# Attention over sequences of unequal length: ScalarE copies pair 2 in two-tile halves, and SyncE reads two rows of its table at once

## The chip, the core and the metric

The kernel runs on one NeuronCore of a Trainium2 chip. The core has TensorE (PE: matmuls, and weight loads, PEld), VectorE (DVE), ScalarE (ACT), GpSimd (POOL) and SyncE (SP), which issues most of the DMAs. The engines run their own instruction streams and wait for each other on semaphores. The metric is the device time of one execution in microseconds.

## What is computed

32 sequences of 64 to 511 valid rows, 8 heads of 64 columns. Rows past a sequence's length are zero in the output.

```python
for b in range(batch):                       # 32
    x_b = x[b, :lengths[b]]                  # up to 512 rows x 512
    q, k, v = np.split(x_b @ w_qkv, 3, axis=-1)          # each split into 8 heads of 64
    scores = 64 ** -0.5 * (q @ k.T)          # per head
    attn = softmax(scores)                   # per row
    output[b, :lengths[b]] = attn @ v        # heads side by side
```

## The kernel before

The sequences are sorted by length, longest first, and taken two at a time. A pair gets a class N (its length rounded up to 32 rows) and T = N/128 rounded up, the number of 128-row tiles. For every class there is a body with two halves, one for each sequence of the pair (h = 0, 1). While half h runs the attention of its sequence, it projects the next sequence, g = 1 - h. All engines have a copy of each body and branch to it by the class, which they read from a table.

Inside a half the heads go in four pairs. What TensorE does, in order, is a string of tokens; for T = 2:

```python
2: "S S B0 b1 A0 A1 B2 S S V1 b3 A2 O A3 R3 X3 V0",
```

`S` is the scores of one pair (pairs 1, 2, 3 of this sequence, then pair 0 of the next), whose exponential ACT takes. `B` and `b` project Q and K of one pair of the next sequence into one bank of PSUM, a0 and a1 in turn; a capital means that DVE copies the bank to `qkT`, a small letter that ACT does. `V` projects one tile of V into such a bank, and DVE copies it to `v_aug` (where the last tile has up to 64 rows, in two instructions, lines 531 and 532). `A` is attention times V of one pair into the area `pav`. The results of A0 and A1, and of A2 and A3, are normalised together by DVE (a reciprocal, then two multiplications): the first norm behind A1, the second at `R3 X3`. `O` is ACT's store of the first two pairs' output.

A group waits on a semaphore `e_<bank>` until the last reader of its bank is through (`acquire`), and raises `f_<bank>_<engine>` for the engine that reads it. So `b3` waits until the copy of `B2` has freed a0, `V0` until the copy of `V1` has freed a1, and `b1` of the next half until the copy of `V0` has. `A2` writes the area that the first norm reads. Before the change it has no wait of its own for that: `b3` stands ahead of it on TensorE and waits for a copy that stands behind the norm on DVE.

SP moves the data. In a two-tile half it waits until TensorE is done with the old xT (`s_xtf`), transposes the next x (two DMAs, line 1379), stores two pairs of output (line 1302) and loads x for a later sequence (lines 1390 and 1394). Which sequences these are it reads from a table in SBUF, `steps`, one row of four registers for each half (`read_step`, lines 1474 and 1475): an address step and a blocking `TENSOR_LOAD`. `steady` is the path of most two-tile bodies, without branches inside. One-tile bodies take their transposes through a staging area (line 1513), from which GpSimd copies them to xT (line 1710).

Of the kernel before, what the change touches and what calls it, by code (L numbers as in the profile page):

```python
# [152 lines left out]
def kernel(  # L153
# [9 lines left out]
    B, MAXS, D = x.shape  # L163
# [7 lines left out]
    def sb(name, shape, dt):  # L171
        return nc.alloc_sbuf_tensor(name, shape, dt).ap()

    def sem(name):
        return tc.alloc_semaphore(name)
# [20 lines left out]
    rank = sb("rank", [B, 1], FP32)  # L196
# [11 lines left out]
    steps = sb("steps", [1, B, 4], I32)  # L208
# [62 lines left out]
    halves_av = ("v0", "v1")  # L271
# [3 lines left out]
    free = {b: sem(f"e_{b}") for b in banks + halves_av + ("x0",)}  # L275
# [6 lines left out]
    def acquire(pr, b):  # L282
        if pr.busy.get(b):
            pr.take("pe", free[b])
            pr.busy[b] = False
# [262 lines left out]
    def attnv(pr, h, i, T, late=False, b=None, qts=None):  # L548

        for s_ in ("s0", "s1"):  # L550
            if pr.pair[s_] == i or T == 1 and pr.pair[s_] is not None:
                acquire(pr, s_)
        for v in halves_av if b is None else (b,):
            acquire(pr, v)
        va = v_aug[h]
        if b is not None:
            jobs = [(2 * 74 * k, i, qt) for k, qt in enumerate(qts)]
        elif T == 1:
            jobs = [(74 * 2 * j, j, 0) for j in range(NPAIR)]
        elif T == 4:  # L560
            jobs = [(256 * qt, i, qt) for qt in range(T)]
        else:
            jobs = [(74 * (4 * qt + 2 * (i % 2)), i, qt) for qt in range(T)]
        mms = []
        for o0, j, qt in jobs:
            for par in range(2):
                o = o0 + par * (HD + 1 if T == 4 and b is None else 74)
                into = pav if b is None else area[b]
                for kt in range(T):
                    mms.append(  # L570
                        mm(
                            into[:, o : o + HD + 1],
                            ep[:, j, par, kt, qt * P : (qt + 1) * P],
                            va[:, kt, 2 * j + par, :],
                            kt == 0,
                            kt == T - 1,
                        )
                    )
        if b is None and T in (2, 3) and i % 2 == 0:
            acquire_carry(pr, mms)  # L580
            return
        on = onat[h]
        if b is not None:
            n = len(qts)
            res = into[:, 0 : 2 * 74 * n].rearrange("p (t a d) -> p t a d", a=2, d=74)
            dst = on[:, i // 2, qts[0] : qts[0] + n, P * (i % 2) : P * (i % 2 + 1)]
            dst = dst.rearrange("p t (a d) -> p t a d", d=HD)
            sh, fin = [n, 2], i % 2 == 1 and T - 1 in qts
        elif T == 4:
            res = pav.rearrange("p (j n) -> p j n", n=256)[:, :, 0 : 2 * (HD + 1)]  # L590
            res = res.rearrange("p j (a d) -> p j a d", d=HD + 1)
            dst = on[:, i // 2, :, P * (i % 2) : P * (i % 2 + 1)]
            dst = dst.rearrange("p t (a d) -> p t a d", d=HD)
            sh, fin = [NT, 2], i % 2 == 1
        else:
            sh, fin = [2, 4] if T == 1 else [T, 4], True
            res = pav[:, 0 : 74 * sh[0] * 4].rearrange("p (b j d) -> p b j d", j=4, d=74)
            if T == 1:
                dst = on[:, :, 0, :].rearrange("p b (j d) -> p b j d", d=HD)
            else:  # L600
                dst = on[:, i // 2, 0:T, :].rearrange("p t (a d) -> p t a d", d=HD)
        r0 = 2 * qts[0] if b is not None else 0
        rv = rcp[:, i, r0 : r0 + sh[0] * sh[1]].rearrange("p (j a) -> p j a", a=sh[1])
        num, den = res[..., 0:HD], res[..., HD]
        name = "av" if b is None else b
        close(pr, name, "dve", mms, False)
        each = T == 4 or b is not None

        def recip():
            opens = i % 2 == 0 and (b is None or 0 in qts)  # L610
            for j in (0, 1) if T == 1 else (i // 2,) if not each or opens else ():
                pr.take("dve", s_od[h][j], 16)
            pr.take("dve", full[(name, "dve")])
            pr.add("dve", lambda e: e.reciprocal(out=rv, in_=den).then_inc(s_r, 1))  # L614

        def mult():
            pr.take("dve", s_r)

            if T == 1:
                cuts = [(slice(0, 2), 0)]  # L620
            elif b is not None:
                whole = [] if h else [k for k, t in enumerate(qts) if t < T - 1]
                cuts = [(slice(0, len(whole)), None)] if whole else []
                cuts += [(slice(k, k + 1), t) for k, t in enumerate(qts) if k not in whole]
            elif h == 0:
                cuts = [(slice(0, T - 1), None), (slice(T - 1, T), T - 1)]
            else:
                cuts = [(slice(t, t + 1), t) for t in range(T)]

            def fn(e):  # L630
                for w, t in cuts:
                    ops = dict(
                        out=dst[:, w], in0=num[:, w],
                        in1=rv[:, w].unsqueeze(3).broadcast_to(list(num[:, w].shape)),
                    )
                    if t is None:
                        ins = e.tensor_tensor(op=ALU.mult, **ops)
                    else:
                        ins = e.scalar_tensor_tensor(  # L639
                            scalar=now[0][:, 1, t : t + 1], op0=ALU.mult, op1=ALU.mult, **ops  # L640
                        )
                if fin:
                    ins.then_inc(s_of[h][i // 2], 1)
                if b is not None:
                    if fin:
                        ins = e.memset(small, 0.0)
                    ins.then_inc(free[b], 1)

            pr.add("dve", fn)
            if b is not None:  # L650
                pr.busy[b] = True

        todo = {"R": recip, "X": mult}
        if not late:
            for fn in todo.values():
                fn()
        return todo
# [5 lines left out]
    def spread_last(pr):  # L663
# [15 lines left out]
    ORDER = {  # L679
# [3 lines left out]
    }  # L683
    DENSE = "K2 q2 D E1 E3 I1 H3 D k0 c A0 Q0~ A1 D V2 O V1 A2 D A3~ V0"
    FOUR = "S E1 S G1 S E2 S G2 S E0 S E3 S G0 G3 S S A0 Z0 V1 +A1 S S Z1 V3 +A2 S O S V0 +Z2 S A3 Z3 S S V2"
# [648 lines left out]
    with nc.Block() as block:  # L1334

        @block.sync
        def _(e):
# [11 lines left out]
            rank = e.alloc_register("rank")  # L1349
# [90 lines left out]
            for more in range(EARLY):  # L1440
# [7 lines left out]
            cur = regs[e.engine][1]  # L1448
            steps_r = [
                [e.alloc_register(f"{r}{h}") for r in ("ahead", "own", "steady")] for h in range(2)  # L1450
            ]
            steps_r = [[ahead, cur, own, flag] for ahead, own, flag in steps_r]
# [17 lines left out]
                    e.reg_mov(owed, 0)  # L1470
                nc.switch_bb(out_, parent=top)

            def read_step(h):
                e.reg_load(steps_r[h], steps[
                    0:1, bass.ds(e.snap(rank, min_val=0, max_val=B - 1), 1), :])

            def steady(N):

                k, top = CLASSES.index(N), nc.cur_bb
                yes, no = f"even_b{N}", f"even_x{N}"  # L1480
                e.br_cmp(steps_r[0][3], CLASSES.index(P), yes, no, "IS_LT")
                nc.switch_bb(yes, parent=top)
                for h in range(2):
                    if h:
                        read_step(h)
                    wait_dec(e, s_xtf[h])
                    to_xT(h, N, 2)
                    if h == 0:
                        pay_owed(f"{N}e", False)
                    else:  # L1490
                        pay(0)
                    wait_dec(e, s_xc[1 - h])
                    load(1 - h, 5, N, index(h, 0))
                    e.reg_add(rank, rank, 1)
                e.reg_mov(owed, 1)
                e.reg_mov(flat, 1)
                e.br_cmp(cur, k, f"sp_b{k}", f"even_z{N}", "IS_EQ")
                nc.switch_bb(f"even_z{N}", parent=top)
                e.br(f"sp_x{k}")
                nc.switch_bb(no, parent=top)  # L1500
# [50 lines left out]
            def body(e, N):  # L1551
                T = -(-N // P)
                read_step(0)
                if T == 1:
                    staged(N)
                if T == 2:
                    steady(N)
                for h in range(2):
                    if h:
                        read_step(h)  # L1560
                    top = nc.cur_bb
                    lab, out_ = f"trans_b{N}_{h}", f"trans_x{N}_{h}"
# [265 lines left out]
```

## Time and profile before

| | |
|---|---|
| median of 3 runs | 339.34 us (339.07 to 339.44) |
| the profiled execution | 338.92 us; its span, first to last instruction, 337.2 us |
| granted TensorE clock, mean | 0.994 |
| busy: PE, DVE, ACT, POOL | 321.1, 209.9, 243.0, 67.8 us |
| two-tile halves | 12, from 237.5 to 315.5 us of the span |
| one-tile halves | from 315.5 us to the end |

How to read the rows: in a timeline a row has its start and its length in us, the engine, the line, the operation and the tiles (out <- in), and in brackets how long the engine idled before it and what ended that. Rows of groups have `x` and a count, busy us, mean ns of one, and the idle time ahead of the group. `PEq` and `SPq` are the engines' sequencers; line 306 is the helper that writes every matmul, line 61 and line 1294 are those that write waits. Rows of one line give the shortest, the median and the longest duration in ns. In rows of waits stand the total, the count and the longest in us.

### The profile page before, as it was taken

What the parts mean: (1) busy time and instruction counts of PE and PEld (TensorE: products, weight loads), DVE (VectorE), ACT (ScalarE), POOL (GpSimd) and SP (SyncE); (2) the same over time, 40 slices, a digit from 0 to 9 for tenths busy, and PEclk for the clock granted to TensorE, in tenths of its full rate; (3) what the DMA queues carried; (4) which work ended last, traced back from release to release, by engine and by line L of the source; (5) the groups of instructions that cost most, each with busy time, mean ns of one, the idle gap of its engine ahead of it and who ended that gap; (6) DMA issues with size and microseconds to landing.
All of it is one profiled execution on the core that took longest, in us unless ns stands there. A gap on an engine that the chain in (4) does not pass through costs nothing. (4 is left out here: it accounts for less than half of the span.)

```text
span 337.2 us, 12374 instructions
## 1 busy us (share of the span) xinstructions
PE 321.1 (95%) x4390; PEld 207.9 (62%) x4391; DVE 209.9 (62%) x578; ACT 243.0 (72%) x345; POOL 67.8 (20%) x126
## 2 busy tenths in 40 slices
PE   6999999999999999999999999999999999999881
PEld 2664554465656566565666666777768777777660
DVE  3676567455566567467557655865666667677651
ACT  4578788788888987887977888787767575665531
POOL 3634020202020220220222022202123111313150
PEclk9999999999999999999999999999999999999997
DMA  6966799856555976997788969695897557876522
GB/s 213 352 151 223 194 360 256 309 177 208 169 201 155 259 294 152 260 318 227 218 272 286 216 203 316 184 238 172 228 215 191 161 167 160 201 147 179 174 79 71
DMA packets 82273, 72.11 MB, mean 214 GB/s; under 512 B 40652, under 2 KB 63180, under 8 KB 82196
## 3 DMA queue, kind: packets, MB, share of 16 engines
q1 hardware_dynamic: 70340, 59.61, 63.6%
q10 hardware_dynamic: 11856, 11.54, 9.9%
q8 instruction: 40, 0.66, 0.9%
q14 instruction: 37, 0.30, 0.3%
HBM read 25.32 MB, written 36.70 MB: 184 GB/s over the span
## 5 line engine op out<-in xcount | busy, mean ns | idle before, releaser
L348 ACT ACTIVATE ep<-psc 128x704 f16<-128x704 f32 (+7 forms) x193 | 157.0, 861 | 55.9 <-PE psc L306 38.1
L306 PE MATMUL pa<-xT,w_r 128*128 128x224 f16 (+21 forms) x984 | 122.9, 275 | 5.0 <-PEq L61 3.4
L306 PEld LDWEIGHTS pa<-xT,w_r 128*128 128x128 f16 (+1 forms) x984 | 71.9, 97 | 33.5 <-issue 13.4
L412 DVE CAST qkT<-pa 128x512 f16<-128x512 f32 (+9 forms) x73 | 41.5, 570 | 45.5 <-PE pa L306 42.6
L306 PE MATMUL psc<-qkT 64*128 64x352 f16 (+17 forms) x702 | 68.3, 287 | 0.8 <-PEq L61 0.3
L306 PE MATMUL pa<-w_r,xT 128*128 128x512 f16 (+4 forms) x332 | 57.9, 330 | 0.0
L306 PE MATMUL pav<-v_aug,ep 128*128 128x65 f16 x1254 | 55.0, 194 | 0.4 <-PEq L61 0.4
L306 PEld LDWEIGHTS pav<-v_aug,ep 128*128 128x128 f16 x1254 | 49.0, 98 | 9.0 <-issue 1.6
L306 PE MATMUL pav<-xT,w_r 64*128 64x352 f16 (+12 forms) x392 | 50.8, 307 | 0.0
L380 ACT ACTIVATE ep<-psc 128x960 f16<-128x960 f32 (+3 forms) x48 | 43.4, 961 | 8.8 <-PE psc L306 6.0
L639 DVE SCALAR_TENSOR_TENSOR onat<-pav,masks,rcp 128x128 f32<-128x128 f32 (+2 forms) x124 | 44.4, 396 | 5.0 <-DVE rcp L614 1.9
L1666 POOL MEMSET v_aug<- 128x256 f16 x24 | 7.5, 314 | 187.5 <-POOLq L1294 187.5
L306 PEld LDWEIGHTS psc<-qkT 64*128 64x128 f16 x702 | 26.8, 94 | 28.2 <-issue 18.3
L1660 POOL CAST x<-x_nat 128x1536 f16<-128x1536 f32 (+3 forms) x33 | 42.0, 1272 | 8.0 <-POOLq L1294 7.7
L411 ACT CAST qkT<-pa 128x352 f16<-128x352 f32 (+8 forms) x62 | 28.7, 468 | 15.6 <-ACTq L61 7.8
L435 DVE TENSOR_TENSOR v_aug<-pa,masks 128x512 f16<-128x512 f32 (+1 forms) x46 | 30.7, 672 | 13.8 <-PE pa L306 13.5
L306 PEld LDWEIGHTS pav<-xT,w_r 64*128 64x128 f16 (+1 forms) x392 | 26.6, 94 | 12.3 <-issue 1.3
L306 PEld LDWEIGHTS pa<-w_r,xT 128*128 128x128 f16 (+2 forms) x332 | 22.7, 99 | 16.2 <-issue 4.1
L614 DVE RECIPROCAL rcp<-pav 128x8 f32<-128x8 f32 (+2 forms) x69 | 13.5, 196 | 22.5 <-PE pav L306 16.6
L306 PE MATMUL pav<-w_r,xT 128*128 128x512 f16 (+3 forms) x124 | 26.9, 350 | 0.0
L306 PEld LDWEIGHTS pa<-v_aug,ep 128*128 128x128 f16 x538 | 19.7, 98 | 7.1 <-issue 2.9
L306 PE MATMUL pa<-v_aug,ep 128*128 128x65 f16 x538 | 22.3, 194 | 0.0
(84 smaller groups left out, 169.1 us busy)
## 6 DMA issues: line engine op xcount, KB each, us to landing
out_dram<-zt SPq DMA_DIRECT2D x16, 768.0 KB, 6.0
x_nat<-in_x_dram SPq DMA_DIRECT2D x12, 512.0 KB
x_nat<-in_x_dram SPq DMA_DIRECT2D x5, 1024.0 KB
out_dram<-onat ACTq DMA_DIRECT2D x12, 384.0 KB, 4.9
out_dram<-onat SPq DMA_DIRECT2D x12, 384.0 KB, 4.5
x_nat<-in_x_dram SPq DMA_DIRECT2D x17, 256.0 KB, 5.7
out_dram<-onat ACTq DMA_DIRECT2D x16, 256.0 KB, 3.3
x_nat<-in_x_dram SPq DMA_DIRECT2D x4, 768.0 KB
```

Of the source, the lines that this page charges most:

```text
L306: return lambda e: e.matmul(o, lhsT, rhs, start=start, stop=stop)
L348: lambda e: e.activation(out=dst, in_=src, func=AF.Exp, scale=scale),
L380: lambda e, par=par, b=b: e.activation(out=ep[:, i, par, 0:3, 0:N], in_=psc_f[:, par, 0 : 3 * N].rearrange("p (t n) -> p t n", n=N), func= ...
L411: return lambda e: e.copy(out=dst, in_=src)
L412: return lambda e: e.tensor_copy(out=dst, in_=src)
L435: return lambda e: e.tensor_tensor(out=v_aug[h][:, t, lo // HD : lo // HD + n, 0:HD], in0=area[b][:, 0:w].rearrange("p (a d) -> p a d", d=HD),
L614: pr.add("dve", lambda e: e.reciprocal(out=rv, in_=den).then_inc(s_r, 1))
L639: ins = e.scalar_tensor_tensor(scalar=now[0][:, 1, t : t + 1], op0=ALU.mult, op1=ALU.mult, **ops)
L1660: e.tensor_copy(out=x16[h][:, 0:T, :], in_=x_nat[h][:, 0:T, :]).then_inc(s_xc[h], 1)
L1666: e.memset(v_aug[h][:, T - 1, NPAIR:NH, 0:HD], 0.0)
```

## The change

Three edits, all for T = 2:

1. `B2` becomes `b2`: the copy of pair 2 of Q and K goes from DVE to ACT.
2. The first norm of a half (i = 1) ends with a memset of one element on DVE that raises the semaphore of `v0`, a half of `pav`; the next user of the area on TensorE, `A2`, waits for it.
3. SP reads both rows of `steps` at the top of a two-tile body, the second one into spare registers. At the start of the second half two register moves take the place of the read.

```diff
@@ attnv @@
+        back = halves_av[0] if b is None and T == 2 and i == 1 else b
...
-                if b is not None:
+                if back is not None:
                     if fin:
                         ins = e.memset(small, 0.0)
-                    ins.then_inc(free[b], 1)
+                    ins.then_inc(free[back], 1)
 
             pr.add("dve", fn)
-            if b is not None:
-                pr.busy[b] = True
+            if back is not None:
+                pr.busy[back] = True
@@ ORDER @@
-        2: "S S B0 b1 A0 A1 B2 S S V1 b3 A2 O A3 R3 X3 V0",
+        2: "S S B0 b1 A0 A1 b2 S S V1 b3 A2 O A3 R3 X3 V0",
@@ sync @@
-            def read_step(h):
-                e.reg_load(steps_r[h], steps[
-                    0:1, bass.ds(e.snap(rank, min_val=0, max_val=B - 1), 1), :])
+            def read_step(h, at=None, into=None):
+                at = rank if at is None else at
+                e.reg_load(into or steps_r[h], steps[
+                    0:1, bass.ds(e.snap(at, min_val=0, max_val=B - 1), 1), :])
+
+            def read_second():
+                e.reg_add(second[3], rank, 1)
+                read_step(1, second[3], [second[0], cur] + second[1:3])
+
+            def take_second():
+                for k, r in ((0, second[0]), (2, second[1])):
+                    e.reg_mov(steps_r[1][k], r)
+
+            second = [e.alloc_register(f"{r}_second") for r in ("ahead", "own", "steady", "rank")]
@@ steady @@
                     if h:
-                        read_step(h)
+                        take_second()
@@ body @@
                 if T == 2:
+                    read_second()
                     steady(N)
                 for h in range(2):
-                    if h:
+                    if h and T == 2:
+                        take_second()
+                    elif h:
                         read_step(h)
```

The places that the prediction speaks of, in the second half of the body of class 192 when the next pair has class 160. On DVE, from the first norm to the copies of `V1`, before:

```order
L614 RECIPROCAL rcp<-pav 128x8 [waits s_od10,f_av_dve]
L639 ISA [waits s_r]
L639 SCALAR_TENSOR_TENSOR onat_1<-pav,masks,rcp 128x256
L639 ISA
L639 SCALAR_TENSOR_TENSOR onat_1<-pav,masks,rcp 128x256
L412 CAST qkT_0<-pa 128x2x160 [waits f_a0_dve]
L531 ISA [waits f_a1_dve]
L531 TENSOR_TENSOR v_aug_0<-pa,masks 128x4x64
```

The same place with the change, from the norm's last multiplication on:

```order
L640 ISA
L640 SCALAR_TENSOR_TENSOR onat_1<-pav,masks,rcp 128x256
L647 MEMSET small 1x1
L531 ISA [waits f_a1_dve]
L531 TENSOR_TENSOR v_aug_0<-pa,masks 128x4x64
```

And on ACT, from the exponentials of pairs 1 and 2 to the copy of `b3`, with the change:

```order
L348 ACTIVATE ep<-psc 128x2x2x192 [waits f_s0_act]
L348 ACTIVATE ep<-psc 128x2x2x192 [waits f_s1_act]
L411 CAST qkT_0<-pa 128x2x160 [waits f_a1_act]
L411 CAST qkT_0<-pa 128x2x160 [waits f_a0_act]
L348 ACTIVATE ep<-psc 128x2x2x192 [waits f_s0_act]
L348 ACTIVATE ep<-psc 128x2x2x160 [waits f_s1_act]
L411 CAST qkT_0<-pa 128x2x160 [waits f_a0_act]
```

The copy that waits for `f_a0_dve` behind the norm has left DVE, where a memset of `small` stands in its place now; on ACT it waits for `f_a0_act` ahead of the exponential of pair 3. On TensorE, the groups `V1`, `b3`, `A2` and `A3` with the change:

```order
L306 MATMUL pa<-w_r,xT_0 64x256 [waits s_on0,e_a1]
L306 MATMUL pa<-w_r,xT_0 64x256 x7
L306 MATMUL pa<-xT_0,w_r 128x160 [waits e_a0]
L306 MATMUL pa<-xT_0,w_r 128x160 x7
L306 MATMUL pav<-v_aug_1,ep 128x65 [waits e_v0]
L306 MATMUL pav<-v_aug_1,ep 128x65 x7
L306 MATMUL pav<-v_aug_1,ep 128x65 [waits e_s0]
L306 MATMUL pav<-v_aug_1,ep 128x65 x7
```

The order of the groups is the one before; the wait for `e_v0` at the first matmul of `A2` is new. On SP, the steady path of class 192 around the load of x in the first half, before:

```order
L1394 ISA
L1394 DMA x_nat_1<-in_x_dram 64x512
L1494 ISA
L1474 TENSOR_LOAD steps
L1379 DMA_TRANSPOSE xT_1<-x16_1 128x4x128 [waits s_xtf1]
```

And the top of the same body, from the first read to the first transposes, with the change:

```order
L1477 ISA
L1476 TENSOR_LOAD steps
L1480 ISA
L1476 TENSOR_LOAD steps
L1493 COMPARE_AND_BRANCH
L1380 DMA_TRANSPOSE xT_0<-x16_0 128x4x128 [waits s_xtf0]
L1380 DMA_TRANSPOSE xT_0<-x16_0 128x4x64
```

The second `TENSOR_LOAD` has moved from between the load of `x_nat_1` and the transpose into `xT_1` to the top, ahead of the branch and of the first transposes, and has an address step of its own there. At the old place one register instruction is left (line 1485), which also makes the moves.

## The prediction

> **What bounds the kernel now.** I read the page's busy line first, then TensorE's weight loads in the stage of the two-tile halves, the timeline of one half, and the waits and the table reads of SyncE (SP).
>
> ```profile
> PE 321.1 (95%) x4390; PEld 207.9 (62%) x4391; DVE 209.9 (62%) x578; ACT 243.0 (72%) x345; POOL 67.8 (20%) x126
> ```
>
> TensorE (PE) is busy for 95% of the span, ScalarE (ACT) and VectorE (DVE) have room. So a change can only bring what PE idles in the stretch it touches: twelve two-tile halves from 237.5 to 315.5 us. The timeline of the weight loads shows the idle time there (in brackets); of the loads that feed from xT these are the ones behind a V group, token `b3`, then three that begin `b1`.
>
> ```profile
> 263.76 0.80 PEld L306 LDWEIGHTS pa<-xT,w_r 128*128 128x128 f16 x8 [0.20 <-issue]
> ...
> 277.41 0.62 PEld L306 LDWEIGHTS pa<-xT,w_r 128*128 128x128 f16 x8 [0.45 <-issue]
> 283.88 0.61 PEld L306 LDWEIGHTS pa<-xT,w_r 128*128 128x128 f16 x8 [0.23 <-DVE qkT L412]
> 290.00 0.54 PEld L306 LDWEIGHTS pa<-xT,w_r 128*128 128x128 f16 x8 [0.55 <-issue]
> 296.04 0.53 PEld L306 LDWEIGHTS pa<-xT,w_r 128*128 128x128 f16 x8 [0.33 <-DVE qkT L412]
> 302.09 0.54 PEld L306 LDWEIGHTS pa<-xT,w_r 128*128 128x128 f16 x8 [0.57 <-issue]
> 308.13 0.53 PEld L306 LDWEIGHTS pa<-xT,w_r 128*128 128x128 f16 x8 [0.32 <-DVE qkT L412]
> 313.95 0.46 PEld L306 LDWEIGHTS pa<-xT,w_r 128*128 128x128 f16 x8 [0.67 <-issue]
> ...
> 280.93 0.61 PEld L306 LDWEIGHTS pa<-xT,w_r 128*128 128x128 f16 x8 [0.34 <-DVE v_aug L435]
> 293.27 0.53 PEld L306 LDWEIGHTS pa<-xT,w_r 128*128 128x128 f16 x8 [0.33 <-DVE v_aug L435]
> 305.36 0.53 PEld L306 LDWEIGHTS pa<-xT,w_r 128*128 128x128 f16 x8 [0.21 <-DVE v_aug L435]
> ```
>
> Up to 273 us a V group has 512 columns, and 0.20 us is the gap that its longer stream leaves. Behind V groups of 256 columns half of that, 0.10, would be left; the seven `b3` idle 3.12 us in all, so 2.4 us are waits. One of them in the timeline of its half:
>
> ```profile
> 287.84 0.42 ACT L411 CAST qkT<-pa 128x320 f16<-128x320 f32 x1
> 288.04 0.72 PE L306 MATMUL pa<-xT,w_r 128*128 128x160 f16 x8
> 288.61 0.88 DVE L639 SCALAR_TENSOR_TENSOR onat<-pav,masks,rcp 128x256 f32<-128x256 f32 x2 [0.16 <-DVE rcp L614]
> 289.17 1.40 ACT L348 ACTIVATE ep<-psc 128x768 f16<-128x768 f32 x2 [0.90 <-ACTq L61]
> 289.40 0.48 DVE L412 CAST qkT<-pa 128x320 f16<-128x320 f32 x1
> 290.32 0.43 DVE L532 TENSOR_TENSOR v_aug<-pa,masks 64x256 f16<-64x256 f32 x1
> 290.58 0.65 PE L306 MATMUL pav<-v_aug,ep 128*128 128x65 f16 x16
> 291.07 0.38 PE L306 MATMUL pa<-w_r,xT 128*128 128x512 f16 x1
> ```
>
> `B2` (288.04) is done by 288.76, but its copy stands behind the norm of `A1` on DVE and ends at 289.88; `b3` takes its bank at 290.00. ACT is idle for 0.90 us meanwhile.
>
> The second view is SP. It waits on other engines in the first part of the stage (first row below, 238 to 273 us, the second row is 279.6 to 316 us):
>
> ```profile
> SPq L1294 <- SPq L1294: 6.0, 5, 1.7
> ...
> SPq L1294 <- SPq L1294: 0.2, 1, 0.2
> ```
>
> In the last 36 us it waits for 0.2 us. SP issues transposes, stores and loads without a pause there: that stretch is bound by SP's own issue. It ends in the first transpose for the one-tile halves:
>
> ```profile
> DMA to landing us min/median/max: 2.4/3.1/4.6
> 315.76 1.23 SPq L1513 DMA_TRANSPOSE xT<-x  x1
> 320.65 0.61 POOL L1710 COPY xT<-xT 128x512 f16<-128x512 f16 x1 [3.27 <-POOLq L1294]
> 321.40 0.88 PE L306 MATMUL pa<-xT,w_r 128*128 128x96 f16 x17 [1.96 <-PEq L61]
> ```
>
> The landing row covers the eleven transposes from 279.6 to 316 us, and its maximum is the one of 315.76: it lands at 320.4, GpSimd copies it at 320.65, and PE, which had idled for 1.96 us, goes on at 321.40. What PE gains ahead of this point is waited away there, unless SP reaches 315.76 sooner. **The end time follows SP.**
>
> **The copy of pair 2.** Rows by shape over the two-tile stage, and the mark from the whole span:
>
> ```profile
> L411 ACT CAST qkT<-pa 128x448 f16<-128x448 f32 x8 | 4.3, 532 | 1.1 <-PE pa L306 0.4 <-ACTq L61 0.4
> L411 ACT CAST qkT<-pa 128x320 f16<-128x320 f32 x8 | 3.4, 425 | 2.0 <-PE pa L306 1.1 <-ACTq L61 1.0
> L412 DVE CAST qkT<-pa 128x320 f16<-128x320 f32 x8 | 3.9, 486 | 0.7 <-PE pa L306 0.6
> L646 DVE MEMSET small<- 1x1 f32 x28 | 1.7, 59 | 0.0
> ```
>
> Twelve copies leave DVE and cost ACT 0.43 to 0.58 us each. In the half shown ACT can start at about 288.8, when `B2` is through, and end at 289.2. The exponentials behind it, now at 289.17, slip by less than 0.1 us at 160 rows and by 0.1 to 0.25 at 192 to 256 rows or where ACT's class read follows the copy. Nobody waits for that: `A3`, the first to need them, comes after `b3` and `A2`. If this cover were gone, each half would pay the slip. Bank a0 is free at 289.25 instead of 289.9, and `b3` could follow V at 289.55: its 0.45 us goes.
>
> **The mark.** DVE ends the norm at 289.49 (288.61 + 0.88); the memset of 59 ns puts the mark at 289.55. PE meets the new wait at `A2`, now at 290.58, then at about 290.1. So it finds the mark 0.5 us old. Behind it in PE's queue would stand `A2`, `A3` and `V0`; I cost it at nothing.
>
> **What is late next on PE.** `V0` needs bank a1, freed by the copies of V1, which end at 290.75 and do not move. `V0` can come at 290.8 instead of 291.07: of 0.45 us, 0.27 stays, so 0.18 is lost. Taking 0.18 from each of the seven waits (0.35, 0.13, 0.45, 0.23, 0.47, 0.22, 0.57) leaves 1.4. The last norm starts the full wait sooner, so the three `b1` waits shrink as well, by up to 0.5. PE gains 1.4 to 1.9 us, 2.4 at most; the five halves before 273 gain nothing.
>
> **The table reads.** Durations of the reads on SP: all of the two- and one-tile bodies, those from 238 to 286 us, then each up to the last two-tile body (286.5, 299.4 and 310.8 are mid-body reads, 293.2 and 305.9 stand at a top). Before them an issue of SP, for the steps around a read.
>
> ```profile
> 298.87 0.34 SPq L1394 DMA_DIRECT2D x_nat<-in_x_dram  x1
> L1474 SPq TENSOR_LOAD <-steps x16: 298/310/1042, 239.1 to 326.6; - x16
> ...
> L1474 SPq TENSOR_LOAD <-steps x7: 302/309/317, 239.1 to 279.2; - x7
> L1474 SPq TENSOR_LOAD <-steps x1: 1042/1042/1042, 286.5 to 286.5; - x1
> L1474 SPq TENSOR_LOAD <-steps x1: 520/520/520, 293.2 to 293.2; - x1
> L1474 SPq TENSOR_LOAD <-steps x1: 554/554/554, 299.4 to 299.4; - x1
> L1474 SPq TENSOR_LOAD <-steps x1: 310/310/310, 305.9 to 305.9; - x1
> L1474 SPq TENSOR_LOAD <-steps x1: 937/937/937, 310.8 to 310.8; - x1
> ```
>
> Until 279 us SP waits for PE after either read, so moving one costs nothing. In the three bodies after that it is on SP's path, at both places:
> - removed: 1.04 + 0.55 + 0.94 = 2.53 us. The address step before the read goes too, but the register moves take its place.
> - added at three tops: a read and an address step. Between the issue that ends at 299.21 and the read at 299.4 lie 0.2 us, which bounds the step from above; I take 0.14. The read I take at 0.31, like four of the five reads at tops (those in the x7 row are 0.32 at most) and against one of 0.52: 3 x 0.45 = 1.35, less the 0.2 us that SP waits at the first of them, 1.15.
>
> The sum is 1.15 - 2.53 = -1.4 us. A transpose that is issued sooner stands closer behind the loads of x, and may take longer to issue or land; I give 0.3 back: **-1.1 us**. The ends: -1.4 with nothing given back; 3 x (1.04 + 0.2) - 0.2 - 2.53 = +1.0 if the second read at each top costs what the slowest did. The break-even is a read of 0.77 us.
>
> By the Trainium skill (Runtime: NRT & Kernel Launch, Instruction fetch mechanics) a register load takes about 200 ns for each register, 0.8 us for the four of a row, and the estimate would be 3 x 0.94 - 0.2 - 2.53 = +0.1 us. The x16 row, with a median of 0.31 us for four registers, speaks against that.
>
> **The sum.** The profiled execution took 338.92 us (span 337.2), 0.42 under the median of the three runs, 339.34. 338.92 - 1.1 = 337.8, or 338.2 in terms of the median.
>
> **The rivals.**
> - *The late landing goes too* (0.13). 4.6 us against a median of 3.1: if the earlier transpose meets the queues at a better time, 1.5 us more go: 338.2 - 1.5 = 336.7. For it: PE idles 1.96 us at this one place. Against: stores and transposes around it shift along with it.
> - *No change* (0.17). What made the three mid-body reads slow stays with the place: they come right behind loads of x, and the next instruction of SP takes the stall, or the reads at the tops pay the same (the mean of the four slow reads is 0.76: 3 x 0.90 - 0.2 = 2.5 against 2.53). SP is where it was, PE waits its gain away at 321.4: 339.3.
> - *Slower* (0.23). The second read stands ahead of a body's first transposes. If the reads at the tops take more than 0.77 us on average, at 1.04 the price is +1.0: 340.3. PE does not hide it: the transpose issued at 301.4 landed 3.1 us later by its own landing row, at 304.5, and PE's next load from xT began at 304.61 in the timeline:
>
> ```profile
> DMA to landing us min/median/max: 3.1/3.1/3.1
> 304.61 0.54 PEld L306 LDWEIGHTS pa<-xT,w_r 128*128 128x128 f16 x8 [0.24 <-issue]
> ```
>
> - *The change does not do what it says* belongs to the case of no change: `b3` would have to wait for something other than `B2`'s copy. The `<-DVE qkT L412` rows speak against it.
>
> **How the numbers follow.** My forecast has 0.47: 338.2 us, by itself 337.7 to 338.8. A measurement can tell about 0.2%, 0.7 us, from no change. Faster by more: 0.44 of the forecast's 0.47 and the first rival, 0.57. Within 0.2%: the rest of the forecast and most of no change, 0.18. Slower: the slower case and the edge of no change, 0.25. The range runs from 336.4, a little under the late landing's 336.7, to the slower case's 340.3.
>
> **What would show it.** Right: no idle over 0.15 us before the weight loads of `b3`; two reads of about 0.31 us at each two-tile top and none in mid-body; GpSimd's copy at 319.5 or earlier. Wrong: that copy at 320.6 or later; reads of over 0.77 us at the tops; an idle PE before `A2`.

## The result and the profile after

The changed kernel takes 339.04 us (median of 22 runs, 337.12 to 342.07) against 339.49 us of the kernel before in the same series (22 runs, 337.15 to 341.84). The ratio is 0.9995 with a 95% interval from 0.9976 to 1.0014: no change that this measurement can tell. Here and below a ratio sets a kernel's runs against those of before in the same series; it is not the quotient of two medians, and the median of before was 339.2 to 339.5 us, but 338.44 us in the series with fillers and one read. The profiled execution took 338.47 us with a span of 336.7 us, where before's took 338.92 and 337.2. Single runs of one kernel scatter with a standard deviation of about 1.1 us, so differences of one or two runs say nothing here; below, runs are compared by their medians and intervals, and profiles by times counted from the start of the two-tile stage, which is the first score matmul of its first half (+78.27 means 78.27 us after it). That start itself lies anywhere from 237.5 to 239.8 us of the span in the profiles, with no change to the code ahead of it.

The busy line of the page of the changed kernel: VectorE 5 us less, ScalarE 4.6 us more, TensorE the same.

```profile
PE 321.2 (95%) x4390; PEld 208.1 (62%) x4391; DVE 204.9 (61%) x578; ACT 247.6 (74%) x357; POOL 67.5 (20%) x126
```

The timeline of the weight loads, of the changed kernel, at the places that answer to those shown of before (`b3` first, then two of the three that begin `b1`):

```profile
277.70 0.61 PEld L306 LDWEIGHTS pa<-xT,w_r 128*128 128x128 f16 x8 [0.20 <-issue]
284.11 0.61 PEld L306 LDWEIGHTS pa<-xT,w_r 128*128 128x128 f16 x8 [0.20 <-issue]
289.89 0.53 PEld L306 LDWEIGHTS pa<-xT,w_r 128*128 128x128 f16 x8 [0.20 <-issue]
295.79 0.53 PEld L306 LDWEIGHTS pa<-xT,w_r 128*128 128x128 f16 x8 [0.20 <-issue]
301.78 0.53 PEld L306 LDWEIGHTS pa<-xT,w_r 128*128 128x128 f16 x8 [0.20 <-issue]
307.67 0.53 PEld L306 LDWEIGHTS pa<-xT,w_r 128*128 128x128 f16 x8 [0.20 <-issue]
312.94 0.54 PEld L306 LDWEIGHTS pa<-xT,w_r 128*128 128x128 f16 x8
...
281.20 0.61 PEld L306 LDWEIGHTS pa<-xT,w_r 128*128 128x128 f16 x8 [0.22 <-DVE v_aug L435]
293.14 0.53 PEld L306 LDWEIGHTS pa<-xT,w_r 128*128 128x128 f16 x8 [0.15 <-DVE v_aug L435]
```

No `b3` waits for VectorE any more; what is left in six of the seven is a gap of 0.20 us for which the profile names no releaser, the same behind V groups of 256 columns as behind those of 512. The half that answers to the one shown of before, in the timeline of all engines of the changed kernel:

```profile
288.27 0.72 PE L306 MATMUL pa<-xT,w_r 128*128 128x160 f16 x8
288.85 0.88 DVE L640 SCALAR_TENSOR_TENSOR onat<-pav,masks,rcp 128x256 f32<-128x256 f32 x2 [0.16 <-DVE rcp L615]
289.03 0.42 ACT L411 CAST qkT<-pa 128x320 f16<-128x320 f32 x1 [0.53 <-PE pa L306]
289.40 1.40 ACT L348 ACTIVATE ep<-psc 128x768 f16<-128x768 f32 x2
289.67 0.06 DVE L647 MEMSET small<- 1x1 f32 x1
289.89 0.53 PEld L306 LDWEIGHTS pa<-xT,w_r 128*128 128x128 f16 x8 [0.20 <-issue]
290.46 0.65 PE L306 MATMUL pav<-v_aug,ep 128*128 128x65 f16 x16
291.13 0.38 PE L306 MATMUL pa<-w_r,xT 128*128 128x512 f16 x1
```

ScalarE copies `b2` at 289.03 while VectorE does the norm of `A1`; the mark stands at 289.73, 0.7 us before `A2` at 290.46. The stage, 77.98 us long before, is 76.37 us long.

The table reads of SP in the changed kernel: those up to 280 us, then the two reads at each of two tops, then the read at the first one-tile top.

```profile
L1476 SPq TENSOR_LOAD <-steps x7: 297/315/558, 239.8 to 279.7; - x7
L1476 SPq TENSOR_LOAD <-steps x2: 298/560/822, 292.8 to 293.8; - x2
L1476 SPq TENSOR_LOAD <-steps x2: 297/437/577, 305.3 to 306.1; - x2
L1476 SPq TENSOR_LOAD <-steps x1: 612/612/612, 315.7 to 315.7; - x1
```

The second read of each of these pairs takes 0.30 us; the first now takes 0.82 and 0.58 us. The end of the stage, in the timelines of SP, GpSimd and TensorE:

```profile
310.08 1.83 SPq L1395 DMA_DIRECT2D x_nat<-in_x_dram  x1
312.77 1.21 SPq L1380 DMA_TRANSPOSE xT<-x  x1
316.54 1.78 SPq L1525 DMA_TRANSPOSE xT<-x  x1
319.68 0.61 POOL L1725 COPY xT<-xT 128x512 f16<-128x512 f16 x1 [2.98 <-POOLq L1295]
320.43 1.52 PE L306 MATMUL pa<-xT,w_r 128*128 128x96 f16 x32 [1.66 <-PEq L61]
324.25 0.93 PE L306 MATMUL pa<-xT,w_r 128*128 128x96 f16 x18 [0.90 <-PEq L61]
```

TensorE still idles 1.66 us at the staged transpose (called the gate below), but resumes at 320.43 instead of 321.40. A second wait of 0.90 us, at 324.25, is new: it is for the second staged transpose.

### The profile page after: what moved, and what is told of

The parts are those of the page before. It is cut to its first block, busy times and chain, and to the rows that moved or that the text cites. A ratio compares the mean times of both kernels' runs of the same rounds, so it can differ in the third digit from the quotient of the medians.

```text
span 336.7 us, 12392 instructions
## 1 busy us (share of the span) xinstructions
PE 321.2 (95%) x4390; PEld 208.1 (62%) x4391; DVE 204.9 (61%) x578; ACT 247.6 (74%) x357; POOL 67.5 (20%) x126
## 5 line engine op out<-in xcount | busy, mean ns | idle before, releaser
L412 DVE CAST qkT<-pa 128x512 f16<-128x512 f32 (+9 forms) x61 | 35.0, 575 | 47.4 <-PE pa L306 41.4
L411 ACT CAST qkT<-pa 128x320 f16<-128x320 f32 (+8 forms) x74 | 34.5, 470 | 21.2 <-PE pa L306 14.1
```

Of the source, the lines that this page charges most:

```text
L411: return lambda e: e.copy(out=dst, in_=src)
L412: return lambda e: e.tensor_copy(out=dst, in_=src)
```

## The experiments

The diffs in this section are shortened.

**Each part alone.** The first kernel is before with the copy of pair 2 on ScalarE and the mark, and SP as before; the second is before with SP's reads at the tops alone.

```diff
 e1_copy_mark (to before)
-        2: "S S B0 b1 A0 A1 B2 S S V1 b3 A2 O A3 R3 X3 V0",
+        2: "S S B0 b1 A0 A1 b2 S S V1 b3 A2 O A3 R3 X3 V0",
+        back = halves_av[0] if b is None and T == 2 and i == 1 else b   # and the mark
 e2_reads (to before)
+                    read_second()      # at a two-tile body's top
-                        read_step(h)
+                        take_second()
```

> The kernel before with the ScalarE copy and the mark alone; SyncE reads its table as before. Theory G (gate): TensorE's two-tile stage, from the first two-tile scores to the first one-tile scores, shortens from 78.0 us to about 76.4 us, but the first one-tile projection from the staged transpose waits for SyncE, so the idle time of 1.96 us there grows to about 3.5 us and the total stays within 0.2% of before. Rival R (reads): the copy is worth its 1.5 us in the total and the moved reads of the full change ate it; this kernel is faster by about 1.4 us (0.4%).

> The kernel before with SyncE's two reads at the top of a two-tile body alone; VectorE copies pair 2 as before. Theory G: TensorE's two-tile stage stays at 78.0 us (within 0.4), SyncE issues the staged transpose at the same distance from the stage's start as before (78.3 us, within 0.5), because what made the mid-body reads slow falls on the next instruction of SyncE; total within 0.2%. Rival R: SyncE gets later by 0.5 to 1 us, the total slower by as much. Third reading, my forecast's: SyncE is 1.1 us earlier and the total with it.

Measured: the copy alone 338.44 us, ratio 0.9973 (0.9944 to 1.0003); the reads alone 338.62 us, 0.9980 (0.9952 to 1.0008). Neither can be told from no change, and neither shows one part eating the other's gain. The profiles say more: with the copy alone the stage takes 76.24 us, with the reads alone 78.16. But the gate moved in both, from +83.91 to +82.07 by the copy alone, and to +82.06 by the reads alone. The copy alone leaves SP's reads where they were, so the gate does not follow SP's reads only. TensorE idles 1.86 us there, not the 3.5 us that theory G expected. With the reads alone it does not idle at the gate at all:

```profile
320.97 0.40 PE L306 MATMUL psc<-qkT 64*128 64x128 f16 x8
321.30 0.90 PE L306 MATMUL pa<-xT,w_r 128*128 128x96 f16 x17
```

SP issues the staged transpose at +77.54 in that profile, 0.7 to 0.8 us sooner than in two profiles of before, and it has landed when TensorE asks for it.

**SP's second store.** If SP's time sets the gate, relieving SP should let the copy's gain through. First the store moves to ScalarE, at the end of a half, in either kernel:

```diff
 g0_before_store (to before), g1_after_store (to after)
-                        pay(0)                       # SP, and pay_owed at h == 0
+                act_store(pr, h, 1, T)               # ScalarE, end of a two-tile half
```

> The kernel before, with one load taken from SyncE: in two-tile halves ScalarE issues also the second store of output (pairs 2 and 3), at the end of its half. SyncE loses a wait, an address step and a DMA issue in each of twelve halves, about 0.7 us each, 4 us in the six halves where it does not wait. Theory G: SyncE comes to wait for TensorE again, the staged transpose is issued 2 us or more earlier, the 1.96 us at the gate go to under 0.5, and the total falls by 1.5 us (to 0.9955) with the VectorE copy untouched. Rival (the gate is set by the transpose's landing, not its issue): the total stays within 0.2%. If ScalarE's waits for the norm delay its exponentials, the two-tile stage gets longer than 78.0 us instead.

> The changed kernel with the second store of two-tile halves on ScalarE as in g0. Theory G: with the gate open the copy's gain shows: two-tile stage 76.4 us or less, gate under 0.5 us, total 3 us under the kernel before (0.991). Rival R or scatter alone: no more than g0 gives, or 1 us less than the changed kernel.

Measured: 342.13 us (1.0082, 1.0051 to 1.0112) and 340.77 us (1.0035, 1.0002 to 1.0068). ScalarE waits for the last norm of a half, its next exponentials come late, and the stage grows to 82.50 us without the change (in an execution of 345.02 us, the longest of its series) and 78.77 us with it. The change is worth 1.4 us (medians) here, but the kernels are worse ones.

Then the store is left out:

```diff
 n0_before_nostore (to before), n1_after_nostore (to after)
-                store(e, index(h, 2), h, 1, 2)
+                e.nop().then_inc(s_od[h][1], 16)
```

> The kernel before, with SyncE's second store of each two-tile half left out (the rows of heads of pairs 2 and 3 of the two-tile sequences are not written). Gate theory: SyncE has twelve issues fewer, its last 36 us are no longer bound by its own issue, the staged transpose is issued over 1 us sooner and TensorE's idle time there falls from 2 us to under 0.5: 337.3 to 338 us, 1.3 to 2 us less than before. If TensorE waits there for something other than SyncE (the landing, GpSimd), the idle time stays and the time is that of before, 339.3 us.

> The changed kernel with the same store left out. Gate theory: with SyncE out of the way TensorE keeps what the copy on ScalarE saves, so this one is 1.4 to 1.9 us faster than n0_before_nostore (ratio of the two 0.9945 to 0.996), where the change with its stores was worth 0.1 to 0.4 us. If the gate is not what takes the gain, the two differ by what the change is worth with its stores, at most 0.5 us.

Measured: 338.33 us (0.9970, 0.9943 to 0.9996) and 336.99 us (0.9918, 0.9889 to 0.9947), 1.34 us between the two medians; by their means 1.39 with an interval of 0.9 to either side. TensorE does not idle at the gate in either profile; the row of the changed kernel has no idle time in brackets:

```profile
319.21 0.98 PE L306 MATMUL pa<-xT,w_r 128*128 128x96 f16 x19
```

With SP out of the way the copy is worth what TensorE gains in its stage (77.76 to 76.20 us, 1.56), and the last matmul comes 1.6 us sooner as well (+90.89 and +89.28). That points to the passage from this stage to the one-tile halves as what takes the gain. By the times alone it is not shown: with the stores the means of the main series differ by 0.47 us, with an interval of 0.7 to either side, and the two differences are not clear of each other. What in that passage takes it, these two don't tell, since the store was also out of the DMA engines.

**The same kernels again.**

> The kernel before, unchanged, as a further sample. Any theory: its ratio to the kernel before is 1.000, and the interval shows what a comparison of this size can tell. What it adds is a second profile. If the gate theory holds (the staged transpose for the one-tile halves sets when TensorE goes on), the two-tile stage again takes about 78.0 us from its first to its last half, and TensorE idles again by 1 to 2 us at the first projection behind that transpose. If profiles scatter by as much as the change is worth, the start of that stage (237.49 us before, 238.14 after) moves by over 0.5 us with no change to the code ahead of it, and the idle time at the gate comes out anywhere from 0 to 2 us.

> The changed kernel once more. So far 0.9995 with an interval from 0.9976 to 1.0014. If the change brings nothing: 339.3 us. If it brings the 1.1 us of the forecast: 338.2 us, ratio 0.997. In either case the two-tile stage is to be about 1.6 us shorter than before in the profile (76.4 us against 78.0), since the copy on ScalarE is in it; and the second reads at the three last tops take 0.30 us, the first reads there anything from 0.3 to 0.8 us, if SyncE's slowness falls on whichever instruction stands there.

Measured: 339.24 us and 338.81 us, with ratios of 0.9972 (0.9945 to 0.9999) and 0.9982 (0.9959 to 1.0004). The first is the kernel before itself, so a ratio of 0.997 is within what equal kernels show here. The new profiles gave the two observations that carry the explanation. First, the stage: 77.91 and 76.50 us, and the gate at +83.67 and +82.33. Before and after differ by 1.3 to 1.6 us at the gate in every pairing of these four profiles. Second, the last matmul comes 8.71 us behind the gate in both profiles of before, but 9.60 and 10.17 us behind it in those of after. The gain passes the gate and is lost behind it.

In the second profile of after, and in that of the copy alone, TensorE waits for nothing for long behind the gate: the clock is halved. The windows of the copy alone, then of the second profile of after; the first column with a decimal point behind the stretch is its length, then come the busy times of PE, PEld, DVE, ACT and POOL; of the last three numbers the first is the granted TensorE clock (PEclk):

```profile
316.79:320.20 3.41, 1.55 (x24) 0.75 (x21) 1.67 (x3) 1.61 (x2) 0.61 (x1) 1.00 0.60 83
320.20:323.62 3.42, 3.42 (x42) 3.10 (x42) 0.77 (x2) 0.48 (x1) 1.44 (x3) 0.50 0.42 115
```

```profile
318.71:322.13 3.42, 1.60 (x35) 1.29 (x34) 1.29 (x3) 1.02 (x1) 1.16 (x3) 1.00 0.48 134
322.13:325.54 3.41, 3.41 (x34) 1.87 (x31) 1.68 (x4) 0.48 (x1) 0.84 (x2) 0.50 0.03 9
```

And of before, whose windows lie otherwise across the same wait:

```profile
319.78:323.19 3.41, 1.79 (x41) 1.74 (x42) 0.90 (x2) 0.97 (x2) 1.91 (x4) 1.00 0.43 118
```

A window of 3.41 us in which TensorE is busy for 1.55 or 1.60 us is followed by one at half clock, which costs 1.5 us (10.17 and 10.26 us against 8.71 behind the gate); after one with 1.79 us it isn't.

**TensorE kept busy at the gate.** Does that clock explain the scatter, and the missing gain?

```diff
 f0_before_fill (to before), f1_after_fill (to after)
         if T == 1:
+            if N == P and W < N:
+                acquire(pr, "a0")
+                pr.add("pe", lambda e: fill(e, 6))   # six 512-column matmuls on zeros into a0
             start_proj()
```

> The kernel before, with six 512-column matmuls on zeros (6 x 0.216 = 1.3 us, into the free bank a0) put in ahead of TensorE's wait for the staged transpose, in the one half where it idles. Clock theory: the clock is halved for 3.41 us after each 3.41 us window in which TensorE idles more than about half (1.82, 1.86 us: halved; 1.62 us and less: not). With 1.3 of the 1.5 to 2.0 us of idle filled no window comes near that, so the clock stays full up to the last matmul in the profile, and the runs lose their share of about 1.4 us: with it in 2 of 5 profiles, 0.6 us less than before in the mean, 338.7 us, and less scatter. Rival (the profiles with a halved clock are a matter of the records, or of chance elsewhere): 339.2 us as before, scatter as before. If the fillers come late to the transpose they cost up to 0.5 us: 339.7 us.

> The changed kernel with the same six matmuls. Clock theory: full clock to the end, about 8.7 us from the first projection behind the gate to the last matmul (10.2 where the clock was halved), 338.3 us, 0.5 less than the changed kernel. If the gate still takes all that the copy on ScalarE saves, it equals f0_before_fill within 0.3 us; if the change brings the staged transpose earlier as in the profile (its gate 1.4 to 1.6 us sooner in the stage), it is up to 1.4 us faster than f0_before_fill. Rival: 338.9 us as the changed kernel.

Measured: 339.09 us (1.0014, 0.9991 to 1.0038) and 337.87 us (0.9984, 0.9958 to 1.0011). The clock stays full in both profiles, but before does not get faster, and the changed kernel gains no more on before than without fillers. That the halved clock costs much on average is therefore not shown; it costs 1.5 us in executions where it falls. The expected 338.7 us and 338.3 us can't be read off against another series, since before itself stood at 338.44 us in this one. The difference of the two is 1.22 us by medians, 1.00 by means, with an interval of 0.6 to either side. That covers the 1.1 us of the forecast, but also the 0.47 us by which the means differ without fillers, so that the fillers bring out the change's gain is not shown. No changed kernel here that computes all of the output is faster than before in a way that can be told.

**One read instead of two.**

```diff
 o1_one_read (to after)
-                    read_second()
+                    read_both()     # one read of eight registers in place of the two at the top
```

> The changed kernel, with both rows of the table in one read of eight registers at a two-tile top instead of two reads of four. If a read costs by its start, it takes about 0.35 us and each top saves 0.30 plus an address step, some 1.2 us of SyncE's time at the three last tops: the staged transpose comes that much sooner, and the time falls by at most 1.2 us, 337.8 us. If it costs by its registers it takes 0.6 us and nothing changes: 338.9 us. If SyncE's slowness falls on whatever stands there, the read takes 0.6 to 0.9 us at the last tops and the time is 338.9 us too.

Measured: 338.87 us, 0.9995 (0.9964 to 1.0026). The read takes 0.53 to 0.56 us at every top, between the two prices expected, and the staged transpose is issued at +76.73, no sooner than in the second profile of after (+76.70). TensorE idles 1.98 us at the gate in this profile, but that falls across two clock windows, the clock stays full, and nothing is late behind: the last matmul comes 8.68 us behind the gate, as in before.

**What makes the staged transpose land late.** Its times in the profiles, from the start of the two-tile stage. The fetch is the 16 KB packet of the queue of kind "instruction" that falls nearest: the page of the changed kernel counts 40 of them (packets, MB, share of the 16 engines).

```profile
q8 instruction: 40, 0.66, 0.8%
```

| kernel | issue | fetch ends | landing | landing less fetch end | gate | last matmul |
|---|---|---|---|---|---|---|
| before | 78.27 | 81.61 | 82.90 | 1.30 | 83.91 | 92.62 |
| before, second profile | 78.38 | 81.36 | 82.65 | 1.29 | 83.67 | 92.38 |
| before with fillers | 78.38 | 80.91 | 82.44 | 1.53 | 83.45 | 92.16 |
| after | 78.40 | 79.76 | 81.28 | 1.52 | 82.29 | 91.89 |
| after, second profile | 76.70 | 80.10 | 81.31 | 1.21 | 82.33 | 92.50 |
| after with fillers | 78.10 | 79.72 | 81.25 | 1.53 | 82.26 | 91.86 |
| one read | 76.73 | 79.64 | 81.18 | 1.54 | 82.19 | 90.87 |
| copy alone | 76.91 | 79.55 | 81.06 | 1.51 | 82.07 | 92.33 |
| reads alone | 77.54 | 82.20 | 80.82 | - | 82.06 | 91.07 |

In eight profiles the transpose lands 1.2 to 1.55 us after the end of a fetch, wherever between +76.7 and +78.4 SP issued it. Where it is 1.3 or less, fifteen of its sixteen pieces had landed 1.66 to 1.89 us before, and the last one came alone. With the reads alone the fetch began only after the landing, and the landing is 3.3 us behind the issue. The rival is ScalarE's store, issued 0.1 to 0.3 us ahead of the transpose in the three profiles with before's code; in the others it is issued from 1.8 us ahead to 0.6 us behind. The last kernel leaves that one store out:

```diff
 q0_before_noact (to before; the last two-tile half only)
-                act_store(pr, h, 0, T)
+                    pr.add("act", lambda e: e.nop().then_inc(s_od[h][0], 16))
```

> The kernel before, without ScalarE's store of the last two-tile half (256 KB, issued 0.1 us ahead of the staged transpose; the rows of heads of its pairs 0 and 1 are not written). Two accounts of why the staged transpose lands late (4.06 to 4.63 us after its issue in three profiles of kernels with this code). Queue account: it stands behind that store in the DMA engines; without the store it lands 2.4 to 3.3 us after its issue, 80.7 to 81.6 us from the start of the two-tile stage, TensorE idles under 0.8 us there and the time falls by 1 to 2 us, 337.5 us. Code account: it lands 1.2 to 1.55 us after the end of the 16 KB code fetch that runs 2 to 3 us after the first one-tile half begins; the store has no part in it, the landing stays at 82.4 to 82.9 us, the idle time at 1.5 to 2.1 us and the time at 339 us.

The time of 338.79 us (0.9984, 0.9957 to 1.0012) decides nothing. The transpose in the profile does; its own row of the source view:

```profile
L1518 SPq DMA_TRANSPOSE xT<-x x1: 1190/1190/1190, 316.1 to 316.1; - x1
DMA to landing us min/median/max: 2.4/2.4/2.4
```

It lands 2.42 us after its issue, at +80.58, in the queue account's range of 2.4 to 3.3 us. The code account, as I had put it, had the landing stay late and is wrong in this profile; the store seems to have a part, as far as one profile shows. But a fetch began at +80.36, when the transpose was all but through. What fits all fourteen profiles is a race. In the eight of the table the fetch begins 0.1 to 2.5 us after the issue of the transpose, which is still in flight and ends 1.2 to 1.55 us after the fetch. With the reads alone, and in the four where SP has no second store, the fetch begins 3.3 to 4.9 us after the issue, and the transpose has landed by then (2.4 to 3.3 us). With before's code the store ahead of it would decide which of the two it is. That the fetch alone would do it was not tried: no run moved it alone.

## Why the prediction was right, and where not

The time lies in the range from 336.4 to 340.3 us. The likeliest case, 1.1 us less, is a ratio of 0.9968 and lies just outside the interval of the main series, though inside that of the repeat (0.9959 to 1.0004); what is measured is within the 0.2% that the prediction called no change, and that had a chance of 0.18. That the time lies in the range speaks for the range's width, which takes in no change: the gain was made in the stage as forecast, and was lost where the prediction did not look.

- **The copy and the mark: right.** `b3` lost its waits, the mark stands ahead of `A2` (0.7 us, forecast 0.5), `A2` waits for nothing, and ScalarE's exponentials begin 1.13 us behind the first matmul of pair 2, as before (288.04 and 289.17 then, 288.27 and 289.40 now). The stage is shorter by 1.4 to 1.8 us in the pairings of before and after, those with fillers included; forecast 1.4 to 1.9. Two sizes were off and cancel in part. The gap that is left is 0.20, not 0.10 us, and by the starts of TensorE's groups the seven waits were 1.9 us in all, not 2.4. At `V0`, 0.18 us were to be lost each time: in the half shown it comes 0.67 us behind `A2` (290.46 and 291.13), where it came 0.49 us behind before (290.58 and 291.07), so 0.18 us are lost there. But that is so in two of the seven halves; three lose about 0.1 us and two nothing, 0.6 us in all. So 1.3 us are left of the seven waits. The prediction had 1.4, though its own figures, 0.18 taken from each, leave 1.2. The `b1` waits give the rest, 0.4 to 0.5 us.
- **The table reads: 0.6 of the sum.** The five reads from 286 us to the last two-tile body took 3.36, 3.35, 3.20, 2.90 and 2.79 us in five profiles with before's reads (before, its second profile, with fillers, the copy alone, without ScalarE's last store); the four that stand in their place took 1.99, 1.90, 2.09 and 1.98 us (after, its second profile, with fillers, the reads alone). That is 1.1 us less in the mean, where the forecast has 2.53 - 2 x 0.31 = 1.9 less for them. The second reads cost 0.30 us as forecast, but for one of 0.68 us with fillers, whose first read took 0.32. The first reads at the two tops, taken as unchanged at 0.52 and 0.31, took 0.82 and 0.58 us in after: the part of the no-change rival by which the slowness is handed on is true for 0.6 us of it there.
- **"The end time follows SP": the step that failed.** It took the 4.6 us from the issue to the landing as fixed to SP's issue. In eight profiles the landing keeps its distance to the end of a code fetch instead. That fetch begins 1.9 to 2.75 us after the first one-tile half does, so in these profiles it moves with TensorE; whose code it is they do not say. So the gain of the copy was not waited away at 321.4; the gate came 1.4 to 1.8 us sooner with the copy alone (+82.07 against +83.45 to +83.91). GpSimd's copy, the mark that was set for this step, came at 319.68 us, between the 319.5 of right and the 320.6 of wrong.
- **What took the gain: none of the rivals.** From the gate to the last matmul both profiles of after, that with fillers and that of the copy alone lost 0.9 to 1.5 us of what they had won, in two ways. With SP late at the end of the stage (the x load of 1.83 us and the staged transpose of 1.78 in the rows above; the profile with fillers shows the same), the second staged transpose is issued late as well and TensorE waits 0.9 us for it. Or the wait at the gate falls into one clock window, and 1.5 us go there. The profile with one read shows neither and keeps its gain (+90.87). How often each falls is not known. From the start of the stage to the last matmul the four profiles of after, fillers and one read among them, take 91.8 us in the mean, the three of before 92.4: 0.6 us of the 1.6, which is the size of the 0.45 us between the medians (0.2 us by the ratio). The scatter of the profiles is as large, so the split is an account of these executions, not of the mean over many.
- **The late landing** had a chance of 0.13 as chance meeting of queues. It is systematic in before (4.63, 4.27 and 4.06 us), and would have been the better place to look.

## What to carry to other kernels

Before a gain on one engine is declared lost at a later wait, find what that wait's own end hangs on: compare its place in two or three profiles counted from the same event, for a landing that keeps its distance to another engine's event, not to its issue, moves with that engine. A transfer's long landing time is a lead, not a constant. And where single runs scatter by 1 us, a 1 us change is read from the stages of the profiles and from pairs of kernels that differ in it alone, not from one comparison of times.

## What the runs showed of the hardware

**Transposes that occupy SP for long overlap code fetches.** In twelve profiles (all but those with the store on ScalarE), from 40 to 83 us behind the start of the two-tile stage, 54 of 144 transposes occupied SP for over 1.3 us (1.2 otherwise); 49 of those 54 overlap a 16 KB fetch of the instruction queue, and 19 of the 90 others do. That is an overlap seen in profiles; no run moved a fetch. The load of x that took 1.83 us above overlaps one too, in the DMA view of 309.8 to 311.6 us of the changed kernel:

```profile
q8 instruction: 1, 0.02, 5.4%
```

The slow table reads are something else: of 29 reads of four registers that took over 0.45 us, 22 overlap none. By the Trainium skill (Runtime: NRT & Kernel Launch, Instruction fetch mechanics) an engine's code is refilled in 16 KiB blocks through a DMA queue of its own, and the cost is mostly hidden. The size agrees; of transfers in other queues, which here are stretched during such a fetch, that section says nothing.

**The clock is halved for less than an idle window.** Windows of 3.41 us in which TensorE idled for 1.82 us or more were followed by half clock, in the two shown and at the ends of the kernels (1.84, 1.85 and 1.88 us in three of them); windows with 1.62 us and less were not. The Trainium skill (TensorE: Matmul & The Clock Gate, The HAM clock gate) has the same length of a free-running window, and half clock after an idle one; here 1.82 us of idle time in a window of 3.41 us were enough.
